# Three edits of order in an fp32 encoder layer: where the long input is normalised, which queue stores, and when the first gate pair's raw weights are read

## The chip, the cores and the metric

The kernel runs on one core of one Trainium2 chip. The core has five engines that run side by side, each through an instruction list of its own, in order: TensorE (PE, matrix products; the loading of its stationary operand is a row of its own, PEld), VectorE (DVE), ScalarE (ACT), GpSimd (POOL) and SyncE (SP). They hand work to each other through semaphores. Transfers between the chip's memory (HBM) and the core's SBUF are issued by an instruction of one of the engines and then run on 16 DMA engines. The metric is device time in microseconds (us) of one execution; lower is better.

## The reference, cut to what matters

One encoder layer is applied with the same weights to two inputs: a long one (1024 tokens) and a short one (512), each with 16 learned meta tokens ahead. The model width is 1024.

```python
n = rms_norm(h, g_mix)
qa, ka, va, qb, kb, vb = split(n @ w_in)               # one combined projection
oa = gqa(rope(rms_norm(qa)), rope(rms_norm(ka)), va)   # grouped-query attention
ob = rms_norm(diff_attention(rope(qb), rope(kb), vb))  # two softmax maps, their difference
h = h + concat(oa, ob) @ w_out
n = rms_norm(h, g_ffn)
gate = conv3(n @ w_ff_gate)                            # width 3 over tokens, zero padded
h = h + (gelu(gate) * (n @ w_ff_up)) @ w_ff_down
h = rms_norm(h, g_final)[:, 16:]
```

Everything is fp32.

## The kernel before, in words

**Split operands.** An fp32 product is made of three matmuls on operands in a shorter format: each operand is split into a high part (a cast on ScalarE, L114) and a low part (a subtraction on VectorE or GpSimd, L115), and `mm3` (L121 to L123) adds high x high, high x low and low x high into one PSUM tile. So a weight must arrive by DMA (`w_f`), be cast (`w_hi`) and be subtracted (`w_lo`) before TensorE can use it. Some weights are split beforehand, stored in DRAM and read as finished parts: `wo` (part of `w_out`) and `wg` (the first pair of gate blocks).

**Stages.** Tokens lie along the free dimension, features on the partitions, in 8 blocks of 128 (`KT`). In order: the projection of the short input (from 0 to about 150 us); attention of the short input, merged with the projection of the long one (to about 520 us); attention of the long input merged with the short one's output projection and FFN (to about 1319 us); the long input's output projection, `mixer_out_long`, merged with the last piece of the short one's FFN (to about 1442 us); the long input's FFN, `conv_glu_long` (gate, up and down products, to the end).

**Projection.** `projection(s)` has a prelude: it loads the 8 blocks `x`, makes `xhi` on ScalarE (L234) and `xlo` on VectorE (L235), squares `x` on ScalarE (L238), and needs the sum of the squares over all features for the RMS norm (`rstd`). For the short input the sum is made by TensorE, with a matrix of 1/1024 as the stationary operand (L241, 16 products in all, two column chunks of 256 and 272). For the long one GpSimd adds the blocks to a tile `acc` (L245, three column chunks of 384, 384 and 272, seven times), and TensorE sums `acc` over the partitions at the end (L255). In the program's text the whole prelude of the long input stands behind the projection of the short one, but its passes on ScalarE, VectorE and GpSimd were free to come early. Once `rstd` is known, the rotary tables `rope` are scaled by it (L366, GpSimd). Then come the products tile by tile, with their norm (L312 to L333), rotation (L272, L275) and split.

**mixer_out_long** takes the tokens in parts. For each it reads `m` and the residual `res` (L712), the weights `w_hi`, `w_lo` from `wo` (L167), and stores each block of the result `h` (L729). The short input's FFN ends in the same stretch and stores its result `yT` (L845). All of these DMAs are issued by SyncE, in one list: an issue waits until its tile is free or its data is there, and all later issues wait behind it.

**conv_glu_long** goes through pairs of feature blocks f0, f0 + 2, and so on; each product of a pair against the tokens is made with 7 half-size products in place of 8 (`winograd`), on sums of weights `w_s` and sums of activations `t`. The first pair's gate product reads its weights finished from `wg` (L920) and runs in two column chunks (342 and 170); the sums `t_hi`, `t_lo` of the second chunk are still made while the first runs (`late`, with its rows at L667 and L680). The convolution needs the gate at one further token (the last meta token, kept as `x0`): ScalarE multiplies the raw weight `w_f` by it (L970, 8 instructions, tile `prod`), VectorE sums (L972, tile `acc`), and TensorE sums over the partitions (L989). This needs the raw `w_gate`, which the finished parts don't replace, so the first pair reads 2 x 512 KB for it as well. After the gate come its convolution (L996 on ScalarE, L997 and L999 on VectorE), the GELU and the up product with its raw weight `w_f2`.

**What sets the order.** The program is written as generators that are merged; a scheduler then places each engine's list, and a helper, `behind(g, ins)`, keeps an instruction behind another one of the same engine without any data between them.

Of the kernel before, what the change touches and what calls it, by code (L numbers as in the profile page):

```python
# [196 lines left out]
def projection(ctx, g, s, side, tag, tag2):  # L197
# [11 lines left out]
    products = []  # L209
# [9 lines left out]
    first = load_weight(g, wp, g.w_in[KA], ahead=1 + s)  # L219

    with tc.tile_pool(name=f"ps{s}", bufs=2, side=side, reuse_waits="tile") as sp:
        if s == 1:
            ms = [g.psum.tile(P, cw, tag2) for _, cw in chunks]
        else:
            acc = sp.tile([P, n], F32, name="acc", bufs=1)
        for k in range(KT):
            x = sp.tile([P, n], F32, name="x", tag="x", bufs=2 if s == 0 else 8)
            nc.sync.dma_start(out=x, in_=g.xT[s][k * P:(k + 1) * P, :])
            gk = g.vec[:, V_GMIX + k:V_GMIX + k + 1]
            with ExitStack() as order:  # L230

                for ins in g.norm_of_short:
                    order.enter_context(tc.issue_after(ins))
# [3 lines left out]
                sq = acc if k == 0 and s == 0 else x  # L237
                nc.scalar.activation(sq, x, AF.Square)  # L238
            if s == 1:
                for ps, (c0, cw) in zip(ms, chunks):  # L240
                    nc.tensor.matmul(ps, lhsT=g.ones_d, rhs=x[:, c0:c0 + cw], start=k == 0, stop=k == KT - 1)  # L241
            elif k:
                for c0, cw in chunks:
                    a = acc[:, c0:c0 + cw]
                    nc.gpsimd.tensor_tensor(out=a, in0=a, in1=x[:, c0:c0 + cw], op=ALU.add)  # L245
        c0, cw = chunks[0]
        first_ps = g.psum.tile(P, cw, tag)
        with behind(g, *g.short_products):
            products.append(dense(g, first_ps, first, xhi, xlo, c0, cw))
        for i, (c0, cw) in enumerate(chunks):  # L250
            if s == 1:
                ps = ms[i]
            else:
                ps = g.psum.tile(P, cw, tag2)
                nc.tensor.matmul(ps, lhsT=g.ones_d, rhs=acc[:, c0:c0 + cw], start=True, stop=True)  # L255
            last = rsqrt_newton(g, sp, rstd[:, c0:c0 + cw], ps, cw)
        scaled = nc.vector.tensor_scalar(out=rstd, in0=rstd, scalar1=-0.5, scalar2=None, op0=ALU.mult)
        g.norm_of_short = [last, scaled.ins]
# [8 lines left out]
    def rotary(j, c0, cw, src, cos, sin):  # L267
# [7 lines left out]
        nc.gpsimd.tensor_tensor(out=u, in0=u, in1=w, op=ALU.add)  # L275
# [9 lines left out]
    pending = []  # L285
# [11 lines left out]

    tab = load_tables(0)
# [28 lines left out]
    def values(j):  # L327
        w = load_weight(g, wp, g.w_in[j], ahead=1 + s, lo_engine=nc.gpsimd if s == 0 else None)
# [36 lines left out]
    for tb in tab:  # L365
# [1061 lines left out]
```

## Time and profile before

| what | value |
|---|---|
| median of 3 runs | 2130.71 us (2130.59 to 2131.08) |
| the profiled execution's own time | 2127.9 us |
| its span in the profile | 2126.1 us |
| mean granted TensorE clock | 0.989 |
| HBM read, written | 211.13 MB, 82.85 MB |

A row of the groups and of the timeline reads: line, engine, operation, output tile from input tiles, shape; "x12" is the number of instructions. A row of the waits says which engine and line waited for which other one, with the total in us, the number of times and the longest. SPq is SyncE's queue of DMA issues. The view of windows gives for each stretch the busy time of each engine, then the mean clock that TensorE was granted (PEclk, 1.00 is full), the busy share of the DMA engines and their GB/s. In the chain of waits each row has its start, its length and what it was.

### The profile page before, as it was taken

The page shows a single profiled execution, that of the slowest core. Times are in us where ns is not written, and L with a number is a line of the kernel's source. Part 1 is how long each engine was busy: PE and PEld are TensorE (multiplying, and loading weights), DVE is VectorE, ACT ScalarE, POOL GpSimd, SP SyncE. Part 2 cuts the span into 40 slices and gives each one's busy share as a digit, 9 for nine tenths or more (in the row PEclk, how much of TensorE's full clock was granted, in tenths as well). Part 3 has the DMA queues.
Part 4 walks back from the last instruction along what each step waited for, and adds up shares of the span by engine and source line. Part 5 has one row for each costly group of instructions (what it writes and reads, how often), then busy time and mean ns, then how long its engine had stood idle before and what let it go on. Part 6 is the DMA issues. An engine that isn't in the chain of part 4 may idle for free.

```text
span 2126.1 us, 35236 instructions
## 1 busy us (share of the span) xinstructions
PE 2040.4 (96%) x12302; PEld 1822.3 (86%) x12302; DVE 1725.0 (81%) x3786; ACT 1156.0 (54%) x2253; POOL 560.8 (26%) x494
## 2 busy tenths in 40 slices
PE   6999999998999999999999999988999999999998
PEld 6988888997887989999989999987887777778877
DVE  6878889767879788888998885578778878879886
ACT  6635566544567556666666765345444444435454
POOL 4653233453112000000000000421544444330112
PEclk9999999999999999999999999999999999999999
DMA  7563435457621322223352225996322232247443
GB/s 255 176 203 130 119 111 171 153 178 236 209 79 56 105 75 67 74 82 118 104 187 88 86 97 147 276 290 217 107 100 90 101 113 84 94 167 260 119 126 127
DMA packets 171426, 296.31 MB, mean 139 GB/s; under 512 B 21456, under 2 KB 90608, under 8 KB 170736
## 3 DMA queue, kind: packets, MB, share of 16 engines
q1 hardware_dynamic: 171248, 294.05, 42.5%
q8 instruction: 97, 1.59, 0.3%
q14 instruction: 81, 0.66, 0.1%
HBM read 211.13 MB, written 82.85 MB: 138 GB/s over the span
## 4 chain that ended last, share of the span: by engine, by line
PE 76%; DVE 12%; DMA 4%; issue 3%; ACT 2%; POOL 1%; SPq 0%; DVEq 0%; ACTq 0%; POOLq 0%
PE ps_mm L121 17%; PE ps_mm L123 17%; PE ps_mm L122 17%; PE ps_t L456 5%; PE ps_s L431 3%; PE ps_s L432 3%; PE ps_s L122 2%; PE ps_s L123 2%; PE ps_s L121 2%; DVE p L433 2%; PE ps_o L471 2%; DVE w_lo L115 1%; PE ps_o L470 1%; DVE acc L972 1%; DMA m<-oT 1%
## 5 line engine op out<-in xcount | busy, mean ns | idle before, releaser
L121 PE MATMUL ps_mm<-xhi,w_hi 128*128 128x258 f32 (+3 forms) x1264 | 383.1, 303 | 12.3 <-ACT xhi L114 5.6
L122 PE MATMUL ps_mm<-xlo,w_hi 128*128 128x258 f32 (+3 forms) x1264 | 378.4, 300 | 0.3 <-POOL xlo L115 0.3
L123 PE MATMUL ps_mm<-xhi,w_lo 128*128 128x258 f32 (+3 forms) x1264 | 377.1, 299 | 0.3 <-DVE w_lo L115 0.3
L433 DVE TENSOR_SCALAR_CACHE_REDUCE p<-ps_s 114x344 f32<-114x344 f32 (+4 forms) x562 | 257.8, 489 | 28.1 <-PE ps_s L432 16.8
L114 ACT CAST pt_hi<-ps_t 128x512 fp32r<-128x512 f32 (+6 forms) x360 | 169.6, 484 | 180.8 <-PE ps_t L456 153.3
L121 PEld LDWEIGHTS ps_mm<-xhi,w_hi 128*128 128x128 f32 x1264 | 239.6, 190 | 18.3 <-ACT xhi L114 7.8
L438 ACT ACTIVATE p<-p,nm 114x1040 f32<-114x1040 f32 (+5 forms) x212 | 214.8, 1013 | 70.5 <-DVE nm L436 69.3
L115 DVE TENSOR_TENSOR w_lo<-w_f,w_hi 128x1024 fp32r<-128x1024 f32 (+1 forms) x182 | 195.2, 1080 | 67.3 <-ACT w_hi L114 66.8
L122 PEld LDWEIGHTS ps_mm<-xlo,w_hi 128*128 128x128 f32 x1264 | 240.0, 190 | 1.9 <-POOL xlo L115 0.8
L123 PEld LDWEIGHTS ps_mm<-xhi,w_lo 128*128 128x128 f32 x1264 | 239.4, 190 | 1.2 <-DVE w_lo L115 0.5
L114 ACT CAST w_hi<-w_f 128x1024 fp32r<-128x1024 f32 (+1 forms) x199 | 167.4, 856 | 79.3 <-PE ps_mm L122 52.2
L115 DVE TENSOR_TENSOR pt_lo<-ps_t,pt_hi 128x512 fp32r<-128x512 f32 (+4 forms) x312 | 172.0, 562 | 42.5 <-ACT pt_hi L114 40.9
L115 POOL TENSOR_TENSOR a_lo<-gate,a_hi 128x256 fp32r<-128x256 f32 x44 | 43.1, 981 | 540.9 <-ACT a_hi L114 521.0
L431 PE MATMUL ps_s<-k,q 128*114 128x348 f32 (+4 forms) x552 | 182.7, 336 | 3.2 <-DVE p L433 3.0
L456 PE MATMUL ps_t<-ident,p 128*128 128x128 f32 (+7 forms) x1188 | 182.4, 269 | 0.9 <-DVE nm L436 0.5
L121 PE MATMUL ps_s<-xhi,w_hi 128*128 128x256 f32 (+4 forms) x480 | 148.2, 311 | 23.2 <-DVE t L333 7.7
L432 PE MATMUL ps_s<-k,q 128*114 128x348 f32 (+4 forms) x552 | 170.3, 313 | 0.0
L456 PEld LDWEIGHTS ps_t<-ident,p 128*128 128x128 f32 (+7 forms) x1188 | 139.9, 135 | 29.1 <-issue 6.8
L123 PE MATMUL ps_s<-xhi,w_lo 128*128 128x256 f32 (+4 forms) x480 | 147.0, 307 | 3.2 <-DMA w_lo<-wo 3.0
L122 PE MATMUL ps_s<-xlo,w_hi 128*128 128x256 f32 (+4 forms) x480 | 148.7, 311 | 1.2 <-DVE xlo L115 0.5
L122 PE MATMUL ps_mm<-t_lo,w_hi 128*128 128x512 f32 (+2 forms) x368 | 142.8, 388 | 1.4 <-DVE t_lo L115 1.4
L121 PE MATMUL ps_mm<-t_hi,w_hi 128*128 128x512 f32 (+2 forms) x368 | 142.8, 388 | 0.0
(273 smaller groups left out, 5269.7 us busy)
## 6 DMA issues: line engine op xcount, KB each, us to landing
w_f<-w_gate SPq DMA_DIRECT2D x46, 512.0 KB, 3.4
w_f<-w_up SPq DMA_DIRECT2D x44, 512.0 KB, 3.3
w_f<-w_in SPq DMA_DIRECT2D x36, 512.0 KB, 4.0
a_f<-act SPq DMA_DIRECT2D x62, 256.0 KB, 2.7
w_f<-w_down SPq DMA_DIRECT2D x22, 512.0 KB, 3.4
act<-a_t SPq DMA_DIRECT2D x44, 256.0 KB, 2.1
a<-w_down SPq DMA_DIRECT2D x40, 256.0 KB, 5.4
w_hi<-wo SPq DMA_DIRECT2D x36, 256.0 KB, 5.2
```

The lines of the kernel that those rows point to most:

```text
L114: return (nc.scalar.copy(hi, src).ins, (lo_engine or nc.vector).tensor_tensor(out=lo, in0=src, in1=hi.bitcast(F32), op=ALU.subtract).ins)
L115: (lo_engine or nc.vector).tensor_tensor(out=lo, in0=src, in1=hi.bitcast(F32), op=ALU.subtract).ins)
L121: nc.tensor.matmul(ps, lhsT=whi, rhs=xhi, start=start, stop=False)
L122: nc.tensor.matmul(ps, lhsT=whi, rhs=xlo, start=False, stop=False)
L123: return nc.tensor.matmul(ps, lhsT=wlo, rhs=xhi, start=False, stop=stop).ins
L431: nc.tensor.matmul(ps, lhsT=q[0], rhs=k[:, c0:c0 + cw], start=True, stop=False)
L432: nc.tensor.matmul(ps, lhsT=q[1], rhs=k[:, c0:c0 + cw], start=False, stop=True)
L433: nc.vector.tensor_scalar(out=p[:, c0:c0 + cw], in0=ps, scalar1=HD ** -0.5, scalar2=-3.0e38, op0=ALU.mult, op1=ALU.max, accum_out=mx[:, i: ...
L438: g.last_exp = nc.scalar.activation(p, p, AF.Exp, bias=nm, accum_out=l).ins
L456: nc.tensor.transpose(tps[:, c:c + M], p[:, k0:k0 + kw], g.ident[:M, :M])
L470: nc.tensor.matmul(o, lhsT=v[:, i, :], rhs=hi, start=i == 0, stop=False)
L471: nc.tensor.matmul(o, lhsT=v[:, i, :], rhs=lo, start=False, stop=False)
```

## The change

**A, the projection.** The long input's prelude is now written between the tiles of the short one: the program advances the short projection by five steps, then in turns the long prelude by one block and the short projection by two steps. The `xhi` and `xlo` passes of a block are kept behind the split of the latest weight, and there are three buffers of `x` in place of two. The sum of squares of the long input is made on TensorE, 24 products with the matrix of 1/1024 (L236 after the change) into three PSUM tiles; the 21 additions on GpSimd and the 6 products at their end are gone. The long input's first weight, its first product and its norm stand behind that, still inside the short projection. The scaling of the rotary tables (L365 after) is kept behind the fifth rotation.

**B, the stores.** `h` (L725 after) and `yT` (L841 after) are issued by ScalarE in place of SyncE.

**C, the first gate pair.** The raw `w_gate` blocks, the sums made of them and the raw `w_up` blocks are now kept behind the last load from `wg` (L919 after).

```diff
-    first = load_weight(g, wp, g.w_in[KA], ahead=1 + s)
+    if s == 1:
+        first = load_weight(g, wp, g.w_in[KA], ahead=2)
...
+        ms = [g.psum.tile(P, cw, t) for t, (_, cw) in zip((tag2, tag2) if s == 1 else ("mm", "mm", "o"), chunks)]
         for k in range(KT):
-            x = sp.tile([P, n], F32, name="x", tag="x", bufs=2 if s == 0 else 8)
+            x = sp.tile([P, n], F32, name="x", tag="x", bufs=3 if s == 0 else 8)
...
-            with ExitStack() as order:
-                for ins in g.norm_of_short:
-                    order.enter_context(tc.issue_after(ins))
+            with behind(g, *(g.splits[-1] if s == 0 else [])):
                 nc.scalar.activation(xhi[k], x, AF.Copy, scale=gk)
                 nc.vector.scalar_tensor_tensor(out=xlo[k], in0=x, scalar=gk,
...
-            if s == 1:
+            with behind(g, *g.short_products[-1:]):
                 for ps, (c0, cw) in zip(ms, chunks):
                     nc.tensor.matmul(ps, lhsT=g.ones_d, rhs=x[:, c0:c0 + cw], start=k == 0, stop=k == KT - 1)
-            elif k:
-                for c0, cw in chunks:
-                    a = acc[:, c0:c0 + cw]
-                    nc.gpsimd.tensor_tensor(out=a, in0=a, in1=x[:, c0:c0 + cw], op=ALU.add)
+            if s == 0:
+                yield 0
...
+            with behind(g, *g.splits[-1]):
+                first = load_weight(g, wp, g.w_in[KA], ahead=1)
...
-    for tb in tab:
-        nc.gpsimd.tensor_tensor(out=tb, in0=tb, in1=rstd, op=ALU.mult)
+    with behind(g, rotated[4]):
+        for tb in tab:
+            nc.gpsimd.tensor_tensor(out=tb, in0=tb, in1=rstd, op=ALU.mult)
...
-                nc.sync.dma_start(out=halves(g.h[j], o, w),
-                                  in_=h[:, j, :2 * w].rearrange("p (x t) -> p x t", x=2))
+                nc.scalar.dma_start(out=halves(g.h[j], o, w),
+                                    in_=h[:, j, :2 * w].rearrange("p (x t) -> p x t", x=2))
...
-                    nc.sync.dma_start(out=yv[:, k + 1 - ob:k + 1, c0:c0 + cw], in_=y)
+                    nc.scalar.dma_start(out=yv[:, k + 1 - ob:k + 1, c0:c0 + cw], in_=y)
...
-                nc.sync.dma_start(out=tl.bitcast(F32), in_=pre[i, part, :, half * H:(half + 1) * H])
+                g.last_load = nc.sync.dma_start(out=tl.bitcast(F32), in_=pre[i, part, :, half * H:(half + 1) * H]).ins
...
-        raw = [load_whole(wp, g, g.w_gate[f0 + i]) for i in range(2)]
...
+        if f0:
+            raw, first_sums = load_gate(f0)
...
+        if f0 == 0:
+            with behind(g, g.last_load):
+                raw, first_sums = load_gate(f0)
+                raw_up = [load_whole(up, g, g.w_up[f0 + i], "w_f2") for i in range(2)]
...
+            p1 = projection(es, g, 1, "right", "s", "t")
+            advance(p1, 5)
+            for _ in range(KT):
+                advance(p0, 1)
+                advance(p1, 2)
+            advance(p0, 1)
+            advance(p1, 2)
+            advance(p0, 1)
+            drain(p1)
```

`load_gate` holds the loads of two raw `w_gate` blocks and the instructions on `prod` and `acc` as they were. The lists of the engines differ in two stretches, up to about 520 us and from about 1319 to 1480 us; elsewhere they are the same.

GpSimd's list at its head, before: the tables, a weight's low part and the sums of squares of the long input stand ahead of the first rotation of the short one.

```order
9 L366 TENSOR_TENSOR rope<-rope,rstd 128x528 x2
10 L115 TENSOR_TENSOR w_lo<-w_f,w_hi 128x1024
11 L245 TENSOR_TENSOR acc<-acc,x 128x384 x2
12 L245 TENSOR_TENSOR acc<-acc,x 128x272
13 L245 TENSOR_TENSOR acc<-acc,x 128x384 x2
14 L245 TENSOR_TENSOR acc<-acc,x 128x272
15 L272 TENSOR_TENSOR u<-t,rope 128x256
```

The same place now: the rotations come first.

```order
9 L268 TENSOR_TENSOR u<-t,rope 128x256
10 L271 TENSOR_TENSOR u<-u,w 128x256
11 L115 TENSOR_TENSOR u<-u,hi 128x256
12 L268 TENSOR_TENSOR u<-t,rope 128x272
13 L271 TENSOR_TENSOR u<-u,w 128x272
14 L115 TENSOR_TENSOR u<-u,hi 128x272
```

The additions have left GpSimd's list. The scaling of tables that now comes later (L365) stands at row 23.

TensorE's list before, inside the last of the first gate pair's 7 products (second chunk of columns, 170): the two sums over the partitions of `acc` (L989) stand in the middle of it, and the up product (512 columns) starts right behind it.

```order
8348 L122 MATMUL ps_mm<-t_lo,w_hi 128x170
8349 L989 MATMUL ps_mm<-ones_d,acc 128x2 x2
8350 L123 MATMUL ps_mm<-t_hi,w_lo 128x170
8351 L121 MATMUL ps_mm<-t_hi,w_hi 128x170
```

The same place now, where the names are the same and L998 is the former L989:

```order
8364 L122 MATMUL ps_mm<-t_lo,w_hi 128x170
8365 L123 MATMUL ps_mm<-t_hi,w_lo 128x170
8366 L998 MATMUL ps_mm<-ones_d,acc 128x2 x2
8367 L121 MATMUL ps_mm<-x_hi,w_hi 128x512
8368 L122 MATMUL ps_mm<-x_lo,w_hi 128x512
```

The sums over the partitions now stand between the last gate product and the first up product.

ScalarE's list around that point now: `prod` is the product with the raw gate weight, `act<-gate` the convolution's first pass, `w_f_19422` the first raw up weight.

```order
1316 L968 ACTIVATE prod<-w_f,x_18438 128x128 x8
1317 L1005 ACTIVATE act<-gate,vec 128x1024 x2
1318 L114 CAST w_hi<-w_f_19422 128x512 x2
1319 L968 ACTIVATE prod<-w_f,x_18438 128x128 x8
1320 L999 ACTIVATE gate<-ps_mm 128x1
```

The second `prod` of the pair has the convolution's two passes and two casts of the up weight ahead of it; before, both stood ahead of the gate's last products.

More of the change, by code (lines that the diff above doesn't have):

```diff
@@ L208, in projection @@
     rstd = xp.tile([P, n], F32, name="rstd")
-    products = []
+    products = g.short_products if s == 1 else []
     def load_tables(which):
@@ L236, in projection @@
                                                in1=xhi[k].bitcast(F32), op0=ALU.mult, op1=ALU.subtract)
-                sq = acc if k == 0 and s == 0 else x
-                nc.scalar.activation(sq, x, AF.Square)
-            if s == 1:
+                nc.scalar.activation(x, x, AF.Square)
+            with behind(g, *g.short_products[-1:]):
                 for ps, (c0, cw) in zip(ms, chunks):
                     nc.tensor.matmul(ps, lhsT=g.ones_d, rhs=x[:, c0:c0 + cw], start=k == 0, stop=k == KT - 1)
-            elif k:
-                for c0, cw in chunks:
-                    a = acc[:, c0:c0 + cw]
-                    nc.gpsimd.tensor_tensor(out=a, in0=a, in1=x[:, c0:c0 + cw], op=ALU.add)
+            if s == 0:
+                yield 0
         c0, cw = chunks[0]
-        first_ps = g.psum.tile(P, cw, tag)
-        with behind(g, *g.short_products):
+        if s == 1:
+            first_ps = g.psum.tile(P, cw, tag)
             products.append(dense(g, first_ps, first, xhi, xlo, c0, cw))
[L250 to L258, printed above, removed]
+        for ps, (c0, cw) in zip(ms, chunks):
+            rsqrt_newton(g, sp, rstd[:, c0:c0 + cw], ps, cw)
+        nc.vector.tensor_scalar(out=rstd, in0=rstd, scalar1=-0.5, scalar2=None, op0=ALU.mult)
+        if s == 0:
+            yield 0
+            with behind(g, *g.splits[-1]):
+                first = load_weight(g, wp, g.w_in[KA], ahead=1)
+            c0, cw = chunks[0]
+            first_ps = g.psum.tile(P, cw, tag)
+            with behind(g, *g.short_products[-1:]):
+                products.append(dense(g, first_ps, first, xhi, xlo, c0, cw))
+            yield 0
     es = ExitStack()
@@ L903, in winograd @@
     nc = g.nc
-    a11, a12, a21, a22 = (w[:, i * H:(i + 1) * H] for w in raw for i in range(2))
+    if pre is None:
+        a11, a12, a21, a22 = (w[:, i * H:(i + 1) * H] for w in raw for i in range(2))
+    else:
+        a11 = a12 = a21 = a22 = s2 = None
     def s_(op, a, b):
@@ L961, in conv_glu_long, with load_gate @@
     first = PARTS[-1][0]
-    for f0 in range(0, NFF, 2):
-        gate = up.tile([P, 2, N + 1], F32, name="gate", tag="gate", bufs=1)
+    def load_gate(f0):
         raw = [load_whole(wp, g, g.w_gate[f0 + i]) for i in range(2)]
-        first_sums = []
+        sums = []
         for i in range(2):
@@ L972, in conv_glu_long @@
             nc.vector.tensor_reduce(out=acc, in_=prod.rearrange("p k c -> p c k"), axis=AX.X, op=ALU.add)
-            first_sums.append(acc)
+            sums.append(acc)
+        return raw, sums
+    for f0 in range(0, NFF, 2):
+        gate = up.tile([P, 2, N + 1], F32, name="gate", tag="gate", bufs=1)
+        if f0:
+            raw, first_sums = load_gate(f0)
         for c0, cw in ((0, first), (first, H - first)) if f0 == 0 else ((0, H),):
-            for i, half, ps, rest in winograd(g, wp, up, x, raw, c0, cw, g.wg if f0 == 0 else None):
+            for i, half, ps, rest in winograd(g, wp, up, x, raw if f0 else None, c0, cw, None if f0 else g.wg):
                 t0 = 1 + half * H + c0
@@ L1004, in conv_glu_long @@
                 nc.scalar.preload_act_table_set(EXP_LN)
-        raw = [load_whole(up, g, g.w_up[f0 + i], "w_f2") for i in range(2)]
+        raw = raw_up if f0 == 0 else [load_whole(up, g, g.w_up[f0 + i], "w_f2") for i in range(2)]
         for i, half, ps, rest in winograd(g, wp, up, x, raw, 0, H):
@@ L1229, in merge, with advance @@
             b = None
+def advance(gen, n):
+    for _ in range(n):
+        next(gen)
 def drain(gen):
```

21 lines of the change are left out of this document (9 added, 12 removed).

## The prediction

> **What bounds the kernel now.** I read the page's totals first, then the waits of TensorE in the two stretches whose lists the change alters, then the granted clock behind each long wait. The page:
>
> ```profile
> span 2126.1 us, 35236 instructions
> ...
> PE 2040.4 (96%) x12302; PEld 1822.3 (86%) x12302; DVE 1725.0 (81%) x3786; ACT 1156.0 (54%) x2253; POOL 560.8 (26%) x494
> ```
>
> TensorE is busy for 96% of the span, so the kernel is its matmuls plus about 86 us of holes and whatever the clock takes. An edit of order can only win holes and clock. The waits of TensorE from 0 to 160 us (engine, tile and line, releaser; us in total, times, longest):
>
> ```profile
> PE ps_s L121 <- DVE t L333: 7.7, 2, 6.6
> ...
> PE ps_s L121 <- DVE t L312: 2.5, 1, 2.5
> PE ps_mm L255 <- DVE rstd L106: 2.5, 1, 2.5
> PE ps_mm L121 <- DVE rstd L106: 2.1, 1, 2.1
> PE ps_t L318 <- DVE v L115: 1.3, 1, 1.3
> ```
>
> The wait of 6.6 ends at 46.33 us; L255 and the L121 with `rstd` stand at 151 to 157 us, where the short projection has run out and the long input's norm isn't ready. The same view from 1360 to 1480 us, the output projection of the long input and its first gate product:
>
> ```profile
> PE ps_s L121 <- DMA w_hi<-wo: 4.1, 3, 2.5
> PE ps_s L123 <- DMA w_lo<-wo: 3.0, 3, 1.7
> PE ps_s L657 <- ACT sq_p L734: 2.2, 2, 1.3
> PE ps_mm L121 <- DMA w_hi<-wg: 1.9, 1, 1.9
> PE ps_mm L122 <- DVE t_lo L115: 1.4, 1, 1.4
> PE ps_s L121 <- ACT xhi L114: 1.0, 1, 1.0
> PE ps_mm L123 <- DMA w_lo<-wg: 0.7, 1, 0.7
> PE ps_s L122 <- DVE xlo L115: 0.5, 1, 0.5
> ```
>
> The rows with tile `ps_s` are the output projection, 10.8 us; those with `ps_mm` the gate, 4.0 us. A hole costs more than itself. These are windows laid behind five holes (PEclk is the number behind the engines' busy times):
>
> ```profile
> 46.33:51.80 5.47, 5.47 (x25) 5.47 (x26) 5.43 (x7) 2.79 (x5) 4.69 (x5) 0.50 0.59 191
> 156.74:160.20 3.46, 3.46 (x11) 3.46 (x12) 1.68 (x3) 0.52 (x1) 0.37 (x2) 0.50 0.88 273
> 1381.91:1387.30 5.39, 5.39 (x24) 5.34 (x24) 3.33 (x7) 2.42 (x5) 1.30 (x2) 0.68 1.03 372
> 1410.50:1414.00 3.50, 3.50 (x14) 3.50 (x14) 0.69 (x1) 0.62 (x1) 0.00 (x0) 0.53 0.08 29
> 1441.30:1444.80 3.50, 3.50 (x11) 3.04 (x12) 0.00 (x0) 2.00 (x7) 0.00 (x0) 0.54 1.08 371
> ```
>
> Lost time is length times (1 - clock): 2.7, 1.7, 1.7, 1.6 and 1.6 us.
>
> **A, the projection.** The chain of waits into the hole before 46.33 us:
>
> ```profile
> 34.92 2.25 POOL acc L245 x2
> ...
> 39.79 3.53 DMA x<-xT
> 43.34 1.17 ACT xhi L234
> ```
>
> A short tile's `t` (L333) waited on VectorE behind `xlo` of the long input, this for `xhi`, this for the next `x`, and this for a buffer that GpSimd's additions had not freed. With the additions gone, three buffers and the passes behind the latest weight split, this chain goes, and the wait for `rstd` at 151 us too, since the norm now stands among the short tiles. Removed: 7.7 + 1.3 of short-tile waits, 2.5 + 2.1 at the end, and 2.7 + 1.7 of clock, together 18.0 us. Added is work on TensorE. The first row below is the timeline's, of 12 such sums for the short input; the second and third are groups of the stretch from 0 to 160 us (busy, mean ns of one, idle before); the fourth is a window.
>
> ```profile
> 15.06 2.83 PE L241 MATMUL ps_t<-x,ones_d 128*128 128x256 f32 x12
> ```
>
> ```profile
> L255 PE MATMUL ps_mm<-acc,ones_d 128*128 128x384 f32 (+1 forms) x6 | 2.4, 486 | 2.5 <-DVE rstd L106 2.5
> ...
> L235 DVE SCALAR_TENSOR_TENSOR xlo<-x,vec,xhi 128x528 fp32r<-128x528 f32 (+1 forms) x16 | 18.6, 1185 | 6.7 <-ACT xhi L234 6.6
> ```
>
> ```profile
> 80.00:100.00 20.00, 20.00 (x152) 19.34 (x151) 16.93 (x34) 10.78 (x27) 9.73 (x12) 1.00 0.52 163
> ```
>
> Twelve rows are six products (two matmul records each) and cover 3 x (256 + 272) = 1584 columns in 2.83 us, 1.79 ns a column; 8 blocks of 1040 columns are 14.9 us. What goes, L255, is 1040 columns or 1.9 us by the same price. So 13.0 us more on TensorE, and the fourth row shows that nothing covers it there: from 80 us on, TensorE is busy all the time. If instead they all fell into holes that remain they would cost 0; I take the full price. The hole of 2.5 at L312 (27 us) lies ahead of the short input's norm; one `xhi` (1.17) and one `xlo` (1.185 on average) may now stand in its way on ScalarE and VectorE: +2.3. **A = 13.0 + 2.3 - 18.0 = -2.7 us**, from -8 (sums half hidden) to +9 (the rival below). GpSimd's saving costs and brings nothing by itself, since it is no longer late. The first weight's low part moving to VectorE and the later table scaling have cover as long as the short tiles keep TensorE full; without it they would cost what L121 with `rstd` waits now, 2.1.
>
> **B, the stores.** In SyncE's queue (first row, its timeline) eight stores took 5.78 us, and the load of `w_hi` that TensorE needed next was issued only behind them (second row, chain of waits) and ended the wait of 2.5 at 1381.91. The third and fourth rows are waits in SyncE's queue from 1310 to 1480 us, in which a store waited for VectorE with all loads behind it; the fifth is a window.
>
> ```profile
> 1370.55 5.78 SPq L845 DMA_DIRECT2D yT<-y x8
> ```
>
> ```profile
> 1377.03 4.84 DMA w_hi<-wo
> ```
>
> ```profile
> SPq L729 <- DVE h L728: 3.6, 4, 2.0
> SPq L845 <- DVE y L842: 3.4, 7, 1.3
> ```
>
> ```profile
> 1420.00:1440.00 20.00, 16.96 (x105) 15.97 (x103) 18.93 (x27) 8.79 (x14) 7.02 (x4) 1.00 0.99 313
> ```
>
> Of the 10.8 us of waits, 4.1 + 3.0 + 2.2 = 9.3 are for transfers that were issued late (`sq_p` comes from `res`), and they drag 4.9 us of clock (the last three windows above). All of it is the bound, 9.3 + 4.9 = 14.2, with the 1.5 of `xhi` and `xlo` at the very best 15.7. Against it stands the fifth row: the DMA engines are at 0.99 there, so an earlier issue partly waits in another place. But change C takes raw weights out of this stretch as well: 2 `w_gate` blocks of the first pair and the 4 that followed early, 3 MB or, at that row's 313 GB/s, 10 us of transfer. I take two thirds of the waits and two of the three clock losses: 6.2 + 3.3, **B = -9.5 us**, between 0 and -15.7. The stores' waits (3.6 + 3.4) move to ScalarE's list, with casts queued behind them; ScalarE is busy for 8.79 of 20 us in the fifth row, which is the cover. Without cover these 7.0 us would come back in the casts.
>
> The Trainium skill ("TensorE: Matmul & The Clock Gate", "Part 1: The HAM clock gate") says that the clock halves after an idle window of about 3.4 us, and that only gaps over about 3 us need care. The windows above differ: 0.68 behind a hole of 2.5 us. By the page no clock would be won in B, -6.2 in place of -9.5.
>
> **C, the first gate pair.** The last two loads from `wg`, SyncE's timeline, the first matmul of the up product in the chain, and the four steps that now stand between the two (ScalarE's and VectorE's timeline, with the landing time of the DMA view):
>
> ```profile
> 1464.16 0.39 SPq L920 DMA_DIRECT2D w_lo<-wg  x1
> ```
>
> ```profile
> 1471.55 0.27 PE ps_mm L121
> ```
>
> ```profile
> w_f<-w_gate SPq DMA_DIRECT2D x4, 512.0 KB, 3.6
> ```
>
> ```profile
> 1472.71 0.61 ACT L114 CAST w_hi<-w_s 128x512 fp32r<-128x512 f32 x1
> 1473.41 2.45 ACT L970 ACTIVATE prod<-w_f,x 128x128 f32<-128x128 f32 x8
> 1475.78 1.23 ACT L996 ACTIVATE act<-gate,vec 128x1024 f32<-128x1024 f32 x1
> ```
>
> ```profile
> 1471.33 2.05 DVE L972 TENSOR_REDUCE acc<-prod 128x128 f32<-128x1024 f32 x1
> ```
>
> Today the gate ends 7.4 us after the last load is issued, with the 1.4 of `t_lo` in it, so 6.0 without. What goes: the waits for `wg` (1.9 + 0.7), whose loads had stood behind raw ones in SyncE's queue, and the wait for `t_lo` (1.4), which stood behind an `acc` on VectorE: 4.0 us. What comes: the sums over the partitions (L998) are now the last thing ahead of the up product, and TensorE's list holds everything behind them. The first raw block lands about 0.4 + 3.6 us after the last load, and its `prod` is done as the gate ends. The second `prod` has on ScalarE a convolution pass ahead of it that needs the gate's last product, and two casts: 1.23 + 2 x 0.61 + 2.45, then the `acc`, 2.05: 7.0 us. Hand-overs and the raw up weight, which lands behind both gate blocks, make it more: 4 x 512 KB at 313 GB/s are 6.7 us, about when the gate ends, so I put 8.3, between 7 and 11. A hole of that size is longer than the 6.6 us one, so its clock is that one's, 2.7. **C = 8.3 + 2.7 - 4.0 = +7.0 us**, between +5 and +10; below nothing only if the order shown did not hold.
>
> **Sum.** -2.7 - 9.5 + 7.0 = -5.2 us. The profiled execution took 2127.9 us, 1.8 more than its span and 2.8 less than the median of the runs; the difference is laid on the median: 2130.7 - 5.2 = 2125.5 us. Over 0.2%, 4.3 us, counts as a difference, so below 2126.4 is faster and above 2135.0 slower.
>
> **The rivals.**
>
> *The output projection is freed wholly* (faster). B is then -15.7, for which speaks that most waits there are for single late loads; against it the DMA share of 0.99. -2.7 - 15.7 + 7.0 = -11.4, 2119.3 us; with A at its best 2114.
>
> *The DMA engines are the bound there, whoever issues.* B brings 0: for it the rows with 0.99 and 1.03, against it that the hole at 1410 us has a share of 0.08 right behind it. -2.7 + 7.0 = +4.3, 2135.0 us, just at the bound of slower. The Trainium skill ("DMA: Bandwidth & Descriptors", "Issuing engines are not separate DMA queues") says that issuing from several engines saves only the issuing time of the sequencer, which speaks for this rival; the 5.78 us of eight stores are such time, so the trace bears it out only in part.
>
> *The sums on TensorE wait* (slower). Each of the 8 blocks puts matmuls into TensorE's list that wait for a square on ScalarE, that for the pass behind the weight split, that for the load of `x` (3.53 us above). If TensorE stands there for 1.5 us a block, A becomes -2.7 + 12 = +9.3 and the total +6.8, 2137.5 us. It decides from 9.5 us in all, 1.2 us a block. Three buffers speak against it; that ScalarE and VectorE are the late ones in all waits from 0 to 160 us speaks for it.
>
> **Chances and range.** Forecast 0.5, of it 0.26 faster, 0.22 same and 0.02 slower, since it lies just below the bound; projection freed 0.2, all faster; DMA bound 0.14, 0.08 same and 0.06 slower; sums wait 0.16, 0.03 same and 0.13 slower. Together faster 0.46, same 0.33, slower 0.21. The range goes from the low end of the second case, 2114, to just over the sums that wait, 2138; the forecast's own is 2120 to 2131.
>
> **What would show it.** In the profile after: no wait over 3 us between 30 and 60 us and none for `rstd` at the end of the short projection; 14.9 us of L236 in the dense stretch; PE waits for `wo` below 3 us in sum; one wait of 7 to 11 us at L998 for `acc`, with the clock near 0.5 behind it. I am wrong on C if the up product starts within 3 us of the gate's last matmul, on B if the waits for `wo` stay at 7 us, on A if L236 has idle time of several us before it.

## The result

The changed kernel takes 2147.35 us (median of 6 runs, 2144.54 to 2155.0), the kernel before in the same comparison 2130.89 us (6 runs, 2128.42 to 2138.14): the ratio is 1.0076, with a 95% interval of 1.0058 to 1.0093, or 16.2 us slower. The forecast was 5.2 us faster, with a range of 2114 to 2138. The profiled execution took 2147.51 us. The page of the changed kernel, span and engines:

```profile
span 2145.7 us, 35295 instructions
...
PE 2056.0 (96%) x12344; PEld 1834.2 (85%) x12344; DVE 1725.0 (80%) x3786; ACT 1155.4 (54%) x2253; POOL 534.8 (25%) x473
```

TensorE is as full as before and has 15.6 us more busy time, which I put down to the sums of part A and to slower matmuls behind holes. To see where the 19.6 us of span arise, I read the start of the same matmul in both traces (us from the start of the span):

| place | before | after | offset | of that, in this stage |
|---|---|---|---|---|
| first score product of the short attention | 162.1 | 161.1 | -1.1 | -1.1 |
| 201st score product, the long attention has begun | 596.4 | 602.0 | +5.6 | +6.7 |
| first output projection matmul with 344 columns | 1356.1 | 1363.2 | +7.1 | +1.5 |
| first gate matmul | 1442.1 | 1453.5 | +11.4 | +4.3 |
| end of the last gate matmul | 1471.6 | 1480.7 | +9.1 | -2.3 |
| first up matmul | 1471.4 | 1491.1 | +19.7 | +10.6 |
| end of the span | 2126.1 | 2145.7 | +19.6 | -0.1 |

(The score products are those with tile `q`, the 10 with `halo` left out. The 1.5 us lie in a stretch whose lists are the same; what one profile can vary is shown with the experiments.) Part A loses in the attention behind it, B in the output projection, and C between gate and up. The waits of TensorE from 0 to 161 us now:

```profile
PE ps_s L121 <- ACT xhi L230: 7.3, 1, 7.3
PE ps_s L121 <- DVE t L309: 2.5, 1, 2.5
```

The first is the start of the program, as before; the second is the hole ahead of the norm, unchanged at 2.5. The waits of 6.6, 1.3, 2.5 and 2.1 us are gone, as forecast, and the new sums on L236 never wait (the group's last column is 0.0):

```profile
L236 PE MATMUL ps_mm<-x,ones_d 128*128 128x384 f32 x32 | 11.8, 485 | 0.0
...
L236 PE MATMUL ps_o<-x,ones_d 128*128 128x272 f32 x16 | 5.0, 392 | 0.0
```

The waits of TensorE from 1320 to 1500 us, output projection, gate and start of up:

```profile
PE ps_mm L998 <- DVE acc L970: 9.4, 2, 5.0
PE ps_s L653 <- DVE h L724: 4.2, 1, 4.2
PE ps_s L653 <- ACT sq_p L730: 3.6, 2, 2.2
PE ps_s L121 <- ACT xhi L114: 3.3, 1, 3.3
PE ps_s L121 <- DMA w_hi<-wo: 2.9, 2, 2.2
PE ps_s L123 <- DMA w_lo<-wo: 1.5, 2, 1.2
PE ps_mm L123 <- DMA w_lo<-wg: 0.8, 1, 0.8
```

The waits for `wo` fell from 7.1 to 4.4, those for `wg` from 2.6 to 1.2 (0.8 and one of 0.4). In their place stand waits for ScalarE's `xhi` and for VectorE's `h`, and 9.4 us at L998. What ScalarE did is in its timeline:

```profile
1400.88 9.36 ACTq L841 DMA_DIRECT2D yT<-y  x8
1410.33 0.52 ACTq L725 DMA_DIRECT2D h<-h  x1
1410.90 0.49 ACT L579 ACTIVATE sq<-h 128x344 f32<-128x344 f32 x1 [10.19 <-DMA yT<-y]
1411.68 0.52 ACTq L725 DMA_DIRECT2D h<-h  x1
1412.25 1.23 ACT L114 CAST xhi<-m 128x340 fp32r<-128x340 f32 x3 [0.86 <-DMA yT<-y]
```

For 9.4 us ScalarE did nothing but issue eight `yT` stores. Its next pass found ScalarE idle for 10.2 us, and the casts `xhi` of the next part stood behind it; TensorE's waits at 1409 and 1422 us come behind them. The run with `yT` back on SyncE, below, has neither. The chain of waits between gate and up:

```profile
1474.28 7.32 DMA w_f<-w_up
1481.59 1.46 ACT prod L968 x5
...
1484.09 1.23 ACT act L1005
1485.32 0.39 ACT w_hi L114
...
1486.25 2.45 ACT prod L968 x8
1488.72 1.91 DVE acc L970
...
1490.68 0.59 PE ps_mm L998 x2
```

These are the forecast's steps (convolution, casts, second `prod`, second `acc`), but one more stands ahead of them. The chain's first row names the last raw load; what ScalarE waited for are the two raw gate blocks, issued from 1472.19 us on, which took 8.3 us to land (the DMA view of 1472 to 1476 us). So the first `prod`, too, starts only as the gate ends (ScalarE's timeline), and the convolution passes ahead of the second are two:

```profile
w_f<-w_gate SPq DMA_DIRECT2D x2, 512.0 KB, 8.3
```

```profile
1480.61 2.44 ACT L968 ACTIVATE prod<-w_f,x 128x128 f32<-128x128 f32 x8 [10.27 <-DMA w_f<-w_gate]
1482.96 2.36 ACT L1005 ACTIVATE act<-gate,vec 128x1024 f32<-128x1024 f32 x2
```

Behind the second sum the clock is low:

```profile
1491.30:1495.00 3.70, 3.70 (x10) 2.92 (x11) 3.70 (x4) 2.48 (x9) 1.59 (x1) 0.58 0.03 10
```

3.70 x (1 - 0.58) = 1.6 us.

### The profile page after: what moved, and what is told of

The parts are those of the page before. It is cut to its first block, busy times and chain, and to the rows that moved or that the text cites. A ratio compares the mean times of both kernels' runs of the same rounds, so it can differ in the third digit from the quotient of the medians.

```text
span 2145.7 us, 35295 instructions
## 1 busy us (share of the span) xinstructions
PE 2056.0 (96%) x12344; PEld 1834.2 (85%) x12344; DVE 1725.0 (80%) x3786; ACT 1155.4 (54%) x2253; POOL 534.8 (25%) x473
## 5 line engine op out<-in xcount | busy, mean ns | idle before, releaser
L121 PE MATMUL ps_mm<-xhi,w_hi 128*128 128x258 f32 (+3 forms) x1264 | 383.5, 304 | 10.6 <-ACT xhi L114 6.3
L123 PE MATMUL ps_mm<-t_hi,w_lo 128*128 128x512 f32 (+2 forms) x368 | 142.7, 388 | 0.8 <-DMA w_lo<-wg 0.8
```

What stands on the lines that cost most here:

```text
L121: nc.tensor.matmul(ps, lhsT=whi, rhs=xhi, start=start, stop=False)
L123: return nc.tensor.matmul(ps, lhsT=wlo, rhs=xhi, start=False, stop=stop).ins
```

## The experiments

The ratio of each kernel is to the runs of the kernel before on the same chip, with its 95% interval; 0.0010 is 2.1 us. Offsets are those of the table above, in one profile each. One kernel (the first with another mixing ratio, below) came out with exactly the lists of the kernel before; its ratio was 1.0006 (0.9991 to 1.0020) and its offsets went up to 3.0 us. Two others whose lists are still those of the kernel before at 1356 us (part C with two and with five products of cover, below) have +4.5 and -2.0 there. So an offset below about 3 us in one profile says nothing, and at 1356 us and later one below 5 says little. At the 201st score product the nine kernels with the old lists up to there lie between -1.2 and +2.2, and the four with the changed kernel's lists up to there between +3.2 and +7.8.

### The three parts alone

The edit is the diff of the part and nothing else. Part A:

> Part A alone (the long input's prelude between the short tiles, sums on TensorE); stores and first gate pair as before. Theory from the two traces: the short projection itself ends about 5 us of work earlier than before (no 6.6 us hole, sums 15 us), but the attention of the short input, merged with the long projection, gives back 10 us, so about +5 us against before (lag of 5.6 us at 590 us of the span), 2136. Rival: the loss in the attention is an accident of the list in which all three parts stand together; then A alone shows -3 to -5 us, 2126 to 2128.

Ratio 1.0018 (1.0003 to 1.0032), +3.8 us. The attention starts at 160.1 us (-2.1) and its 201st score product has +6.2.

Part B:

> Part B alone (stores of h and yT issued by ScalarE). Theory: the eight yT stores in a row hold ScalarE's own list for about 9 us, the casts of xhi and VectorE's work come late behind it, and TensorE waits 2 to 4 us three times; +3 to +5 us against before, 2134 to 2136. Rival, as predicted: the weight loads on SyncE come earlier and TensorE's waits for wo go, about -6 us, and what the trace of the whole change shows at 1404 to 1426 us comes from part C's loads.

Ratio 1.0053 (1.0034 to 1.0071), +11.3 us: more than the theory said. Its second group of stores, from ScalarE's timeline, and TensorE's longest waits from 1320 to 1500 us:

```profile
1396.59 8.45 ACTq L845 DMA_DIRECT2D yT<-y  x8
1405.76 0.56 ACTq L729 DMA_DIRECT2D h<-h  x1
1406.37 0.49 ACT L583 ACTIVATE sq<-h 128x344 f32<-128x344 f32 x1 [9.93 <-DMA yT<-y]
```

```profile
PE ps_s L657 <- DVE h L728: 4.2, 1, 4.2
PE ps_s L122 <- DVE xlo L115: 2.4, 1, 2.4
...
PE ps_s L121 <- ACT xhi L114: 2.3, 1, 2.3
```

The same picture without part C, so the rival that put it down to C's loads falls. The waits for `wo` are down to 2.0 us (from 7.1), so the loads do come earlier, as forecast. B alone also loses in the gate, which takes 35.3 us in place of 29.5; in the whole change, where C puts the raw loads behind the last one from `wg`, it takes 27.2.

Part C:

> Part C alone (first gate pair's raw blocks behind the last load from wg). Theory: TensorE waits 9 us at the sums over the partitions between gate and up and runs at half clock for some us after it, 13 us in all, against 4 us won in the gate; about +9 us, 2140. Rival: without B the raw blocks' 3 MB leave SyncE's queue in the output projection and win 3 to 6 us there, so only +3 to +5.

Ratio 1.0029 (1.0014 to 1.0043), +6.2 us, between the two. The wait at the sums is there, in TensorE's waits from 1440 us on:

```profile
PE ps_mm L1002 <- DVE acc L974: 7.5, 2, 4.2
```

Nothing is won ahead of the gate (offset +0.2 at its first matmul).

The parts sum to 21.3 us where the whole change has 16.2; with intervals of 3 to 4 us on either side of each that is agreement, or an overlap. B's loss in the gate, which the whole change doesn't have, would account for it; one profile each doesn't show that.

### Which stores cost: `yT` back on SyncE

```diff
-                    nc.scalar.dma_start(out=yv[:, k + 1 - ob:k + 1, c0:c0 + cw], in_=y)
+                    nc.sync.dma_start(out=yv[:, k + 1 - ob:k + 1, c0:c0 + cw], in_=y)
```

> The changed kernel with the yT stores back on SyncE (h stays on ScalarE). Theory: ScalarE's 9 us of issuing go, with them the waits for xhi and h of 2.2 + 3.3 + 4.2 us, so 6 to 10 us less than the changed kernel, about 2139. Rival: the waits come from the DMA engines being full there; then no difference over 2 us.

Ratio 1.0023 (1.0008 to 1.0038) in place of 1.0076: the `yT` stores on ScalarE were worth 0.5%, or 11 us. TensorE's waits from 1380 to 1445 us:

```profile
PE ps_s L123 <- DMA w_lo<-wo: 6.8, 3, 4.2
PE ps_s L653 <- ACT sq_p L730: 2.5, 2, 1.4
PE ps_s L121 <- DVE h L724: 1.2, 1, 1.2
```

The waits of 3.3 us for `xhi` and 4.2 us for `h` are gone, and with SyncE's stores the wait for `wo` is back. The 24 stores of `h` are still on ScalarE, one at a time at about 0.52 us each; no loss is seen from them here.

### Why eight stores take 9 us

In ScalarE's list each DMA waits for one of eight semaphores, DMAHW0 to DMAHW7, and SyncE's loads take turns on the same eight. These are rows of the list of part B alone, with their waits:

```
1321 L845 DMA yT<-y 128x256 [waits DMAHW5_49,DVE_49]
1322 L845 DMA yT<-y 128x256 [waits DMAHW7_49,DVE_49]
1323 L845 DMA yT<-y 128x256 [waits DMAHW1_49,DVE_49]
1324 L845 DMA yT<-y 128x256 [waits DMAHW3_49,Pool_49]
1325 L845 DMA yT<-y 128x256 [waits DMAHW5_49,DVE_49]
```

SyncE's loads take the semaphores between, so the eight stores get four, and the fifth waits for the semaphore of the first, so for the first to land. In the timeline the first, the fourth and the fifth:

```profile
1396.59 0.34 ACTq L845 DMA_DIRECT2D yT<-y  x1
...
1400.58 0.34 ACTq L845 DMA_DIRECT2D yT<-y  x1
1402.28 0.34 ACTq L845 DMA_DIRECT2D yT<-y  x1
```

The last `y` was ready at 1399.3, yet the fifth store goes out 5.7 us behind the first, at 1402.28 us, where the first (5.6 us from issue to landing; the median of the eight is 4.5) lands at 1402.2. The sixth to the eighth go out within 0.3 us of the landings of the second to the fourth. In the kernel before, whose list has the same eight stores on SyncE, each waits for another of the eight semaphores (DMAHW4 to 7, then 0 to 3): there the fifth went out at 1373.07 us, 2.5 us behind the first and before that one had landed (5.8 us after 1370.55). So the cause would be the number of stores in a row, together with a queue that shares its semaphores with another one's loads. If that is so, half as many stores of twice the size (the tile `y` holds two blocks) should cost much less, with the same bytes.

```diff
-        ob = 2 - s
+        ob = 2
...
-                y = op.tile([P, ob, cw], F32, name="y", tag="y", bufs=YB if s == 1 else 4) if k % ob == 0 else y
+                y = op.tile([P, ob, cw], F32, name="y", tag="y", bufs=YB // 2 if s == 1 else 4) if k % ob == 0 else y
```

> Part B alone, with the short input's result stored two blocks at a time (four yT stores of 256 KB a part in place of eight of 128 KB). Theory: each store on ScalarE waits for one of eight DMA semaphores, which SyncE's loads use in turn with it, so from the fifth store on it waits for an earlier transfer to land (8.45 us for eight); four stores then take about 2 to 3 us and B's loss of 11 us mostly goes: within 3 us of before. Rival: the loss comes from the bytes, not from the number of issues (DMA engines full); then it stays at +8 to +11 us.

Ratio 0.9982 (0.9970 to 0.9994): from 11.3 us slower to 3.8 us faster than before, with no byte less. In its timeline four stores take 3.39 us where eight took 8.45:

```profile
1388.84 3.39 ACTq L845 DMA_DIRECT2D yT<-y  x4
```

But which half of this edit wins, the queue or the number? The same tile, all stores on SyncE as in the kernel before:

> The kernel before with the yT stores two blocks at a time, all stores still issued by SyncE. Theory 1: what made part B with four stores faster is mostly the smaller number of issues, each of which waits for one of the shared DMA semaphores, so this is 2 to 4 us less than before too. Theory 2: it is ScalarE's queue, out of the way of the weight loads; then this is within 1.5 us of before.

Ratio 0.9983 (0.9969 to 0.9998), -3.6 us, the same. In SyncE's timeline four stores take 2.98 us in place of 5.78 for eight:

```profile
1376.88 2.98 SPq L845 DMA_DIRECT2D yT<-y  x4
```

So the measured time is theory 1's: the gain comes with the smaller number of stores, and ScalarE's queue adds nothing that can be measured to it, though the interval (-6.6 to -0.4 us) still reaches into theory 2's 1.5 us. With eight stores the queue does matter: ScalarE's cost 11.3 us. The Trainium skill ("DMA: Bandwidth & Descriptors", "Issuing engines are not separate DMA queues") says that issuing DMAs from several engines saves only the sequencer's time; the pair with four stores agrees (0.9982 on ScalarE, 0.9983 on SyncE).

### Part C with its wait covered

The raw up blocks are read ahead of the raw gate blocks, and the sums over the partitions and the convolution are written behind products of the up weight. Against part C alone, the main lines:

```diff
             with behind(g, g.last_load):
-                raw, first_sums = load_gate(f0)
                 raw_up = [load_whole(up, g, g.w_up[f0 + i], "w_f2") for i in range(2)]
+                raw, first_sums = load_gate(f0)
...
+        if f0 == 0:
+            ups = winograd(g, wp, up, x, raw_up, 0, H)
+            head = [next(ups) for _ in range(HEAD)]
         for i in range(2):
             ps = g.psum.tile(P, 2, "mm")
```

With HEAD = 1, two products:

> Part C alone, with the raw up blocks read ahead of the raw gate blocks and the sums over the partitions (and the convolution) written behind the first two products of the up weight. Theory: C's loss is the wait at those sums alone, and the 4 us won in the gate stay: 2 to 5 us less than before. Rival: four raw blocks behind the last load are late for the up product as well, so TensorE waits there for w_up instead; then +3 us or more against before.

Ratio 1.0029 (1.0011 to 1.0047): no better than C alone. The up product now starts 0.6 us behind the gate, so the wait that the rival names isn't there, although the time is the rival's. Two products are not enough; TensorE's longest wait from 1440 us on is

```profile
PE ps_mm L1005 <- DVE acc L974: 4.0, 1, 4.0
```

and from the first up matmul to the end of the span this profile is 10.9 us longer than that of the kernel before, of which the 4.0 are a part; where the rest comes from isn't shown.

With HEAD = 2, five products. In this kernel, in the first of B and C together and in the one with all three parts, the first quarter of the first up pair adds the running sum `u` after two more products have gone into it, so it holds another value; instructions and their sizes stay the same.

> Part C alone with the raw up blocks first and the sums over the partitions behind five products of the up weight. Theory: the 4 us wait that was left with two products of cover goes with its clock, and the 4 us won in the gate stay: 2 to 5 us less than before. Rival: the convolution, now late, holds the up product's results and the next pair (a wait moves into the next 20 us): within 2 us of before.

Ratio 1.0004 (0.9988 to 1.0020). The up product starts on time (offset -0.7) and C's loss is gone, but its gain doesn't show (the gate takes 29.2 us, as before): C by itself is worth nothing here.

### B and C together

> Parts B and C without A, both mended: four yT stores a part-pair (two blocks each), raw up blocks ahead of raw gate blocks, sums over the partitions and convolution behind five products of the up weight. Theory: the output projection wins 4 to 5 us, the gate 4 us, and nothing waits behind it: 6 to 9 us less than before. Rival: what is won ahead of the gate is given back in the gate stage, whose parts arrive at the rate of the DMA engines; then 2 to 4 us less.

Ratio 0.9961 (0.9944 to 0.9979). The same with the additions in their place (each of the first two quarters gets its sum when its product is written):

```diff
+            for _ in range(HEAD):
+                head.append(next(ups))
+                nc.vector.tensor_tensor(out=head[-1][2], in0=head[-1][2], in1=head[-1][3], op=ALU.add)
```

> Parts B and C without A, both mended: stores of h and of two yT blocks at a time by ScalarE, raw up blocks ahead of raw gate blocks, sums over the partitions and convolution behind five products of the up weight, and the first two quarters of the up product completed ahead of that. Theory: 6 to 9 us less than before (4 to 5 in the output projection, 4 in the gate, nothing behind it). Rival: the completions on VectorE come in the way of the convolution and half of it is given back; 2 to 4 us less.

Ratio 0.9958 (0.9933 to 0.9983), 9.0 us less than before, as the theory had it: this is the version that beats both kernels. Offsets: +1.2 at 1356 us, -3.6 at the first gate matmul, -8.7 at the gate's end, -8.0 at the first up matmul. The gate takes 24.3 us in place of 29.5. So B's and C's gains are real once the stores are few and the sums have cover. Alone the two were worth 0.18% and nothing, together 0.42%; that C's loads can run ahead only where the stores don't hold up their queue would explain it, but that isn't shown: the intervals are too wide.

With part A as it is:

> All three parts with B and C mended as in the kernel with B and C alone, A unchanged. Theory: the parts add up, so A's loss of about 4 us against B's and C's gain: 2 to 5 us less than before. Rival: A's later attention shifts what follows; no difference or slower.

Ratio 0.9971 (0.9957 to 0.9984), 6.2 us less than before; part A still has +7.8 us at the 201st score product.

### Part A

What in A costs in the attention? First the product that A moved ahead of it:

```diff
-            with behind(g, *g.splits[-1]):
+            with behind(g, *(g.splits or [()])[-1]):
                 first = load_weight(g, wp, g.w_in[KA], ahead=1)
...
             advance(p0, 1)
             advance(p1, 2)
-            advance(p0, 1)
             drain(p1)
```

> Part A alone, but the long input's first weight and first product stand behind the start of the merge with the short attention, as before the change. Theory 1: the attention of the short input needs the long projection's products to fill TensorE, and A took 3.8 us of them away; with the first product back, the loss in the attention (6 to 10 us) shrinks by 3 us or more. Theory 2: the loss is a matter of how the two lists happen to interleave, so it changes by a few us either way, without relation to that product.

Ratio 1.0064 (1.0043 to 1.0085), worse: theory 1 falls. Then the sums on GpSimd, with a theory of mine that VectorE's lead at 160 us decides:

> Part A alone with the sums of squares back on GpSimd (additions to acc between the short tiles, six products at the end, two buffers of x). Theory: the stretch from 161 to 590 us is bound by VectorE, and what counts there is how much of VectorE's work is done by 160 us (120.6 us in the kernel before, 112.9 in A alone, 109.8 with the first product moved back, for ends of that stretch that lie 0, 6.2 and 11.6 us later); the 12.4 us of sums on TensorE delay the short tiles on which VectorE works. Without them the attention starts some 8 us earlier than before and the lag at 590 us is between -5 and +1. Rival: the order that A makes is bad in itself, whichever engine sums; then the lag stays at +4 us or more.

Ratio 1.0040 (1.0023 to 1.0057). VectorE had done as much by 160 us as in the kernel before; these are windows of that kernel and, in the second fence, of this one (VectorE is the third busy time):

```profile
0.00:160.00 160.00, 136.19 (x981) 131.46 (x982) 120.65 (x202) 84.44 (x151) 88.49 (x94) 0.95 0.64 212
```

```profile
0.00:160.00 160.00, 139.33 (x997) 134.91 (x997) 120.51 (x203) 85.08 (x151) 87.55 (x92) 0.96 0.61 202
```

The attention starts 2.0 us later than before, not 8 us earlier, and its 201st score product has +10.9. That theory falls as well: the loss stays at the rival's +4 or more. Two more edits of A: without its two small constraints, and the sums alone, in the old order:

```diff
-        with behind(g, *(short_splits if j == VA else [])):
+        with behind(g, *[]):
...
-    with behind(g, rotated[4]):
+    if True:
```

> Part A alone without its two smaller constraints (the scaling of the rotary tables behind the fifth rotation, and the load and split of the group A value weight behind a late split of the short input). Theory 1: A's loss in the attention comes from the order of the short tiles' tail and the value weight; it falls by 3 us or more. Theory 2: it comes from the prelude itself standing among the short tiles; no difference over 2 us from A alone (+4 us against before).

Ratio 1.0018 (1.0001 to 1.0035), as A alone.

> The kernel before with only the sums of squares of the long input moved from GpSimd to TensorE (24 products, three buffers of x, the first product behind the norm); its passes stay free to come early, as before. Theory 1: the sums are 12 us of TensorE work, the hole of 6.6 us at 40 us and the one for the norm at 151 to 157 us (9.3 us of clock and wait) go with GpSimd's additions, and the attention's list stays as it was; within 4 us of before. Theory 2: taking the sums to TensorE is by itself what costs in the attention; +5 us or more.

Ratio 1.0044 (1.0028 to 1.0060), the size of theory 2; but with the sums on GpSimd the loss is as large, so the sums on TensorE can't be the whole cause. Here the attention starts 14.4 us earlier and yet its 201st score product is 11.3 us late. Most of the 25.7 us between is work that has moved: between the two places TensorE is busy for 435.0 us, in the kernel before for 414.7.

| kernel | start of the attention | 201st score product | ratio |
|---|---|---|---|
| A alone | -2.1 | +6.2 | 1.0018 |
| A, first product moved back | -1.2 | +11.6 | 1.0064 |
| A, sums on GpSimd | +2.0 | +10.9 | 1.0040 |
| A without small constraints | -0.8 | +6.9 | 1.0018 |
| sums alone on TensorE | -14.4 | +11.3 | 1.0044 |

An earlier start is no gain by itself; with any of these first stages this place in the attention comes later. Last, the mixture of the two lists. At a ratio of 0.8 the scheduler gave the same lists as at 0.9, so this run is the measure of noise told above:

```diff
-R1, R2, R3 = (1.0, 0.9), (1.0, 0.4), (1.0, 20.0)
+R1, R2, R3 = (1.0, 0.8), (1.0, 0.4), (1.0, 20.0)
```

> The kernel before, with only the mixing ratio of the short attention and the long projection changed (0.9 to 0.8), no work moved between the stages. Theory 2 (interleaving decides): the stretch from 161 to 590 us changes by 3 us or more, although all work is the same. Theory 1 (amount of fill decides): it changes by less than 2 us.

At 2.0 the lists differ:

> The kernel before with the mixing ratio of the short attention and the long projection at 2.0 in place of 0.9 (at 0.8 the lists had come out the same; at 2.0 they differ from the first product of the attention on). No work is moved ahead of the attention. Theory (the interleave of the lists decides): the stretch from 161 to 590 us ends 3 us or more later or earlier. Rival (it is what A does ahead of the attention that costs): it ends within 2 us.

Ratio 1.0123 (1.0106 to 1.0140). The attention starts as before (-0.3), and its 201st score product has +16.9: the order in which the same instructions of attention and projection stand can cost more than any edit ahead of them wins.

> Part A alone with the same ratio of 2.0. Theory: A's loss of 10 to 12 us in the attention changes by 3 us or more in either direction, since the lists interleave otherwise. Rival: the lag at 590 us stays at 5 to 7 us.

Ratio 1.0079 (1.0064 to 1.0094), +18.9 at the 201st score product. So the interleave moves A's loss at this place too, here upwards. Yet at 2.0 the kernel with A is 8.6 us faster than the one without (medians of four runs each, and their intervals don't touch), where at 0.9 it is 3.8 us slower: the sign of A's effect goes with the mixture. The two profiles show only 2.9 us of that, behind this place, so where it is won stays open. That A loses by its interleave is thereby likely, but not shown: no version was found in which A's early stage stands with an attention as good as before. Which edit of A upsets the lists stays open.

What the loss looks like is in the windows of 160 to 596 us, before, with the whole change and with A alone:

```profile
160.00:596.00 436.00, 416.38 (x2699) 384.24 (x2699) 348.35 (x1056) 241.24 (x550) 149.30 (x141) 0.98 0.50 161
```

```profile
160.00:596.00 436.00, 408.62 (x2620) 375.67 (x2619) 353.77 (x1042) 238.42 (x543) 148.51 (x142) 0.98 0.49 160
```

```profile
160.00:596.00 436.00, 411.89 (x2613) 379.07 (x2613) 354.59 (x1041) 237.78 (x542) 148.07 (x141) 0.96 0.49 160
```

TensorE stands idle for 19.6 us before, 27.4 with the whole change and 24.1 with A alone. With the whole change the granted clock is that of before, so the loss there is idle time; A alone has a lower clock on top. The clock differs most from 320 to 400 us, again before and with A alone:

```profile
320.00:400.00 80.00, 75.18 (x494) 70.00 (x493) 68.87 (x232) 49.17 (x133) 30.34 (x22) 0.98 0.54 168
```

```profile
320.00:400.00 80.00, 74.95 (x469) 70.25 (x470) 70.92 (x232) 46.74 (x127) 27.82 (x21) 0.90 0.50 159
```

Here TensorE is busy as long but with fewer matmuls (469 for 494), and the granted clock is 0.90: 80 x 0.08 = 6 us. (With the whole change it is 0.94 there.) The holes in that stretch are mostly waits for VectorE, the longest 1.7 us.

## Why the prediction was wrong

**B failed, at the step "ScalarE is busy for 8.79 of 20 us ..., which is the cover".** I took -9.5, and B alone measures +11.3, a miss of 20.8 us. A's is 6.5 (-2.7 and +3.8), C's 0.8 the other way; together 26.5, where the whole change misses its forecast by 21.4 (-5.2 and +16.2). The price of the stores' waits that I moved to ScalarE (7.0 us "without cover") came from how long SyncE had waited for data. What held them on ScalarE was something else: with SyncE's loads taking every second semaphore, the fifth of eight waits for the first to land. An engine whose average load is 44% has no cover for 9.4 us at a stretch, since everything in its list stands behind them. On SyncE the same eight stores had taken 5.78 and 3.96 us, and I carried no such time over to ScalarE. The step that the weight loads come earlier was right in direction (waits for `wo` 7.1 to 4.4, in B alone 2.0), and the two-block kernels show that about 4 us could be had; not from the queue, but from fewer stores.

**A failed in scope.** Its sum ended at 157 us, and up to there it was about right: the holes went, the sums ran without a wait, and the attention starts 1.1 us earlier with some 4 us more of the long input's products done (5 matmuls of 384 columns at 0.18 us and 24 of 272 at 0.13), so 5 us were won where I had 2.7. The difference is the 2.3 us that I put down for the hole at L312, which stayed at 2.5; and the sums took 12.4 us (from the start of each to the next matmul's) where I had 14.9. The step that failed is unspoken: that what is won ahead of the attention is kept behind it. The attention's lists are also made by the change, although no line of the diff touches them, and they lose 6.7 us by the table, 11 us with the work done in advance. Why they do stays open.

**C was right in mechanism, and in its sum partly by luck.** The wait at L998 is 9.4 us where I had 8.3, its clock 1.6 where I had 2.7, and the gate is 2.3 us shorter where I had 4.0. C alone measures +6.2, I had +7.0. The steps behind the gate's end take 10.0 us (1480.7 to 1490.7) where I had 7.0. I let the first `prod` be done by then, by the DMA view's 3.6 us for a raw block; with four of them issued within 4 us it was 8.3, and the `prod` of 2.4 us came behind the gate. I also counted one convolution pass (1.23 us) where the list shown with the change has two (2.36).

**The rivals.** The slower one that I named (sums that wait on TensorE) didn't happen: L236 has no idle time. "DMA bound whoever issues" was the nearest: the pair of two-block kernels shows that with few stores the queue doesn't matter; that bytes are the reason isn't shown, since with eight stores and the same bytes it does matter. The rival that I missed is the one I had priced in a subordinate clause.

## What to carry to other kernels

Before stores are moved to another engine's queue, count how many stand in a row and what their semaphores wait for: here a run of stores longer than the semaphores it got blocked its engine for a landing time, and fewer, larger stores helped on either queue. A stage that follows a changed one in a scheduled program is changed as well; its order has to be compared and priced too. A wait that is moved between two dense stretches needs as much independent work ahead of it as its whole chain is long, here five products and not two.

## What the runs showed of the hardware

Kernels with the same lists up to a place differed there by 6.5 us in one profile each (+4.5 and -2.0 at 1356 us), and two with the same lists throughout by 0.06% in their runs. The granted clock falls without long holes as well: in A alone it was 0.90 from 320 to 400 us with holes of 1.7 us at most, and 0.50 behind one of 1.74 us that ended at 387.57 us:

```profile
387.80:391.20 3.40, 3.29 (x15) 2.77 (x15) 3.02 (x17) 1.66 (x5) 1.46 (x1) 0.50 0.18 43
```

The Trainium skill ("TensorE: Matmul & The Clock Gate", "Part 1: The HAM clock gate") speaks of an idle window of about 3.4 us; the hole here is half of that. Eight stores of 128 KB took ScalarE 8.45 us and four of 256 KB 3.39 us. Two loads of 512 KB with two more right behind them took 8.3 us to land, where the kernel before had a median of 3.6.
